# One PSUM pool and one side of SBUF kept through the MLP of a one-layer trunk, with four pairs' first products ahead

## The chip, the core and the metric

The kernel runs on one core of a Trainium2 chip. The metric is the device time of the program in microseconds (us): the median of three runs before the change was 1617.08 us (1616.24 to 1624.27). Five engines work side by side: TensorE (PE, matmuls), VectorE (DVE), ScalarE (ACT), GpSimd (POOL) and SyncE (SP, which issues most DMA transfers). Each has its own queue and takes its instructions in order; semaphores hold an instruction back until what it reads is written and what it overwrites has been read. Data lies in SBUF (128 partitions), sums of matmuls in PSUM (8 banks of 128 x 512 floats).

## The reference

One layer over 1024 tokens of 1024 features, with an MLP of 4096 features between:

```
h = rmsnorm(x) * (1 + sc1) + sh1
o = concat(stick_breaking_attention(h), sparse_attention(h))    # each group normalised
x = x + ga1 * (o @ w_out)
h = rmsnorm(x, g_mlp) * (1 + sc2) + sh2
x = x + ga2 * (square(relu(h @ w_up)) @ w_down)
return rmsnorm(x, g_final)
```

The shifts, scales and gates come from `silu(c) @ w_mod + b_mod`. The change lies in the last three lines: between the output projection `o @ w_out` and the end of the MLP.

## The kernel before

All products run in pieces of float32: an operand is split into a high part (ACT copies it into a rounded type, L158) and a low part (DVE or POOL subtracts, L159), and each product is three matmuls, high x high, high x low, low x high.

*Output projection and second norm.* `out_tile` takes 128 tokens at a time, in the order 6, 7, 4, 5, 2, 3, 0, 1: matmuls into two PSUM tiles, DVE adds `x` (L998), ACT squares and sums (L999), SP stores the tile to DRAM (`x1d`), POOL computes the reciprocal root, and DVE multiplies the tile by it in place (L1004); the statistics stand in a small tile `st`. `h2_pair` transposes two tiles on PE into PSUM tiles `x2T` (L1030), ACT brings each out with scale and shift into eight tiles `h2f` of features x tokens (L1034), and the columns of tokens 512 to 1023 are split at once into `h2h` and `h2l`. `h2_sums` then forms, for 256 token columns at a time, four sums and differences of quarters of the activations: `s1` on POOL (L1054), three differences on DVE (L1055 to L1057).

*Up product.* The product with `w_up` runs over 16 pairs `p` of two tiles of 128 output features. For each pair the 2 x 2 block product (two halves of 1024 inputs, two of the tokens) is done in seven half-size products instead of eight, each of 4 x 3 = 12 matmuls of 128x128 by 128x512. Their activation operands are `11`, `12` (from `h2h`, `h2l`), `s1`, `s2`, `s3`, `s4` and `22`, split at the head of the MLP part (names `hs`, `hs1`, `h22`) for columns 256 to 511 first and 0 to 255 last. Their weight operands come from two loads per pair, `wrup{p}_0` (blocks 11, 21) and `wrup{p}_1` (12, 22); DVE forms four differences in place in the loaded blocks (L1183, L1184, L1188, L1190), and ACT and POOL split six or seven blocks of 128x512. The first two products (`up_first`: 11 by 11, then 21 by 12, into the same bank `upa`) need no difference. Between the two, ACT copies the bank out (`p1`, in the trace `p`, L93). The five others (`up_rest`: `upb` with t2, t3, t4 and `upd` with t1 and 22) do; DVE adds `p1` to them (L1210, `u` and `c`), ACT applies relu and square, and the results go to DRAM (`ud`). In program order pairs 0 and 1 do their `up_first` first, then pair 0 its `up_rest`; from pair 2 on, the pieces of one pair's `up_first` alternate with those of the pair before. `gate_piece` meanwhile computes the gate `ga2` from `w_mod` on SP and DVE (`m3raw`, two buffers).

*Down product.* Eight groups of 4 feature tiles read `ud` and `w_down` back, split both, and for each of 8 token tiles x 2 halves do 12 matmuls into a bank `dn` (L177 to L179); DVE adds it (L1347). The last group adds the final norm.

*What sets the order.* The program is written through a tile framework: a scheduler places each instruction in its engine's queue by data, buffers and priorities (`early`, with `PRI`), and a pool gives each tag a number of buffers, so that a tile waits until the one that had its buffer has been read. Around the change, the attention's PSUM pool `psb` (tags z, tr, av: 4, 3 and 1 banks) is closed and a pool `psc` (A, B, D: 4, 2, 2) is opened, and SBUF pool `bq` is closed after the activation splits and `gq` opened in its place.

## Time and profile before

| | us | share |
|---|---|---|
| median of 3 runs | 1617.08 | |
| the profiled execution | 1617.77 | |
| its span | 1616.0 | 100% |
| PE busy (matmuls) | 1438.5 | 89% |
| PE weight loads, beside the matmuls | 1181.8 | 73% |
| DVE busy | 1096.7 | 68% |
| ACT busy | 756.3 | 47% |
| POOL busy | 655.0 | 41% |

The span runs from the first to the last instruction; 1.77 us of the execution lie around it. A matmul's record is longer than the distance to the next one, since matmuls are pipelined. Idle time on PE is what the program pays for where PE is the limit; idle time elsewhere costs nothing. Rows of the timeline give in brackets how long the engine was idle before, and whose work ended that.

### The profile page before, as it was taken

Reading aid. Unit: us, or ns where it says so; the run is one execution under the profiler, and the core shown is the slowest. Engines: PE = TensorE matmul, PEld = TensorE weight load, DVE = VectorE, ACT = ScalarE, POOL = GpSimd, SP = SyncE. Lnnn points to the kernel's source line nnn. Section 1 sums busy time; section 2 is a strip of 40 time slices with the busy share of each in tenths; the row PEclk is TensorE's granted clock in tenths of the full one; section 3 lists DMA queues with packets and bytes.
Section 4 is the critical chain, followed back from the end, with each engine's and each line's share of the span. In section 5 each row is a group of like instructions: output and inputs, shape, how many; then the busy total and the mean of one; then the engine's idle time right before and its main releaser. Section 6 shows DMA issues by size and latency. Waiting matters only on the chain.

```text
span 1616.0 us, 20016 instructions
## 1 busy us (share of the span) xinstructions
PE 1438.5 (89%) x7056; PEld 1181.8 (73%) x7056; DVE 1096.7 (68%) x1950; ACT 756.3 (47%) x1474; POOL 655.0 (41%) x489
## 2 busy tenths in 40 slices
PE   4879968887798778999999778999999999999998
PEld 3658747666686657888788656788788788888886
DVE  7878999999957885999644655352335657566534
ACT  5766465433445545888733543445445212121112
POOL 3343223433436556675552564445443222222101
PEclk8999968888799879999989889999999999999999
DMA  9531221322111212211312134344335623223102
GB/s 327 150 92 41 72 53 40 102 69 91 34 40 40 69 56 86 92 60 53 102 56 104 53 98 143 115 134 128 126 124 202 234 78 122 87 93 105 64 7 98
DMA packets 118213, 155.08 MB, mean 96 GB/s; under 512 B 9520, under 2 KB 77144, under 8 KB 118112
## 3 DMA queue, kind: packets, MB, share of 16 engines
q1 hardware_dynamic: 108464, 136.98, 27.0%
q10 hardware_dynamic: 9648, 16.81, 2.8%
q8 instruction: 56, 0.92, 0.2%
q14 instruction: 45, 0.37, 0.1%
HBM read 116.52 MB, written 33.05 MB: 93 GB/s over the span
## 4 chain that ended last, share of the span: by engine, by line
PE 55%; DVE 27%; DMA 5%; issue 5%; ACT 4%; POOL 3%; SPq 0%; DVEq 0%; POOLq 0%; ACTq 0%
PE dn L178 7%; PE dn L179 7%; PE dn L177 7%; DVE tk_jk L504 4%; DVE tk_jk L530 4%; DVE m L710 4%; PE upb L1199 2%; PE upb L1201 2%; PE upb L1200 2%; DVE m2acc L403 2%; DMA wrup<-in_w_up_dram 2%; DMA wm<-in_w_mod_dram 2%; PE avd L645 2%; PE upd L1200 2%; PE upd L1201 2%
## 5 line engine op out<-in xcount | busy, mean ns | idle before, releaser
L178 PE MATMUL dn<-wld,uh 128*128 128x512 f32 x512 | 201.7, 394 | 0.0
L179 PE MATMUL dn<-whd,ul 128*128 128x512 f32 x512 | 201.6, 394 | 0.0
L177 PE MATMUL dn<-whd,uh 128*128 128x512 f32 x512 | 199.7, 391 | 1.8 <-DVE x L1347 1.8
L173 POOL TENSOR_TENSOR wld<-wrd,whd 128x1024 fp32r<-128x1024 f32 x32 | 81.5, 2557 | 238.5 <-ACT whd L172 223.6
L712 POOL TENSOR_TENSOR be<-be,m 128x895 f32<-128x895 f32 (+7 forms) x64 | 89.4, 1400 | 171.5 <-DVE m L710 111.8
L1347 DVE TENSOR_TENSOR x<-dn,x 128x512 f32<-128x512 f32 x128 | 86.6, 685 | 100.9 <-PE dn L179 100.9
L710 DVE TENSOR_TENSOR_SCAN m<-m 128x896 f32<-128x896 f32 (+7 forms) x64 | 98.7, 1548 | 28.6 <-ACT m L708 26.2
L177 PEld LDWEIGHTS dn<-whd,uh 128*128 128x128 f32 x512 | 97.5, 190 | 23.6 <-DVE x L1347 2.2
L178 PEld LDWEIGHTS dn<-wld,uh 128*128 128x128 f32 x512 | 96.5, 189 | 21.1
L172 ACT ACTIVATE whd<-wrd 128x1024 fp32r<-128x1024 f32 x32 | 33.8, 1056 | 166.3 <-PE dn L178 83.8
L179 PEld LDWEIGHTS dn<-whd,ul 128*128 128x128 f32 x512 | 96.6, 189 | 20.1
L159 POOL TENSOR_TENSOR w<-wrup,w 128x512 fp32r<-128x512 f32 x48 | 62.9, 1315 | 118.3 <-ACT w L158 118.3
L159 POOL TENSOR_TENSOR wt<-wrup,wt 128x512 fp32r<-128x512 f32 x64 | 85.6, 1364 | 19.3 <-ACT wt L158 19.3
L159 DVE TENSOR_TENSOR ul<-ur,uh 128x512 fp32r<-128x512 f32 x64 | 79.2, 1261 | 18.2 <-ACT uh L158 16.0
L530 DVE TENSOR_SCALAR_CACHE_REDUCE tk_jk<-mk,tlo,above 128x384 bf16<-128x384 uint16 (+4 forms) x80 | 74.7, 934 | 2.0
L645 PE MATMUL avs<-wts,va 128*128 128x256 f32 (+1 forms) x320 | 56.3, 305 | 19.7 <-DVE ota L663 10.0
L171 DVE TENSOR_TENSOR wrd<-wrd,gate 128x1024 f32<-128x1024 f32 x32 | 47.2, 1476 | 36.6 <-DMA wrd<-in_w_down_dram 36.6
L504 DVE TENSOR_SCALAR_CACHE_REDUCE tk_jk<-mk,thr 128x384 bf16<-128x384 bf16 (+4 forms) x80 | 70.0, 875 | 1.2
L158 ACT ACTIVATE uh<-ur 128x512 fp32r<-128x512 f32 x64 | 37.6, 620 | 69.7 <-PE dn L178 54.5
L645 PEld LDWEIGHTS avs<-wts,va 128*128 128x128 f32 x320 | 48.1, 205 | 26.1 <-DVE ota L663 9.5
L822 POOL TENSOR_TENSOR dl<-dl,dst 128x896 f32<-128x896 f32 (+4 forms) x40 | 51.2, 1296 | 34.7 <-DVE dst L818 24.7
L158 ACT ACTIVATE w<-wrup 128x512 fp32r<-128x512 f32 x48 | 29.7, 626 | 75.4 <-DMA wrup<-in_w_up_dram 40.2
(386 smaller groups left out, 4471.6 us busy)
## 6 DMA issues: line engine op xcount, KB each, us to landing
wrup<-in_w_up_dram SPq DMA_DIRECT2D x32, 512.0 KB, 5.5
ur<-ud SPq DMA_DIRECT2D x32, 512.0 KB, 3.3
wrd<-in_w_down_dram SPq DMA_DIRECT2D x32, 512.0 KB, 4.4
m2raw<-in_w_mod_dram SPq DMA_DIRECT2D x24, 512.0 KB, 4.3
ud<-c ACTq DMA_DIRECT2D x48, 256.0 KB, 2.1
wm<-in_w_mod_dram SPq DMA_DIRECT2D x24, 256.0 KB, 6.0
x<-in_x_dram SPq DMA_DIRECT2D x8, 512.0 KB, 6.3
wrdq<-in_w_in_dram SPq DMA_DIRECT2D x8, 512.0 KB, 4.8
```

Source lines behind the costliest of these rows:

```text
L158: A.activation(hi, src, AF.Copy)
L159: (lo_eng or V).tensor_tensor(lo, src, hi.bitcast(F32), op=OP.subtract)
L173: (lo_eng or G).tensor_tensor(lo, raw, hi.bitcast(F32), op=OP.subtract)
L177: T.matmul(ps, ah, bh, start=start, stop=False)
L178: T.matmul(ps, ah, bl, start=False, stop=False)
L179: T.matmul(ps, al, bh, start=False, stop=stop)
L504: V.tensor_scalar(jk[:, :widths[b]], src or sc[b], t, 0.5 - TOPK, op0=op, op1=OP.add, accum_out=c)
L530: V.tensor_scalar(jk[:, :widths[b]], mk[b].bitcast(U16), tlo[:, j:j + 1], above[:, j:j + 1], op0=OP.is_ge, op1=OP.add, accum_out=cnt[0][:, ...
L645: T.matmul(dst, vv, rhs, start=kt == 0 and l == 0, stop=half and l == 1)
L710: V.tensor_tensor_scan(m[:, :n][:, ::-1], m[:, :n][:, ::-1], m[:, :n][:, ::-1], 1.0, op0=OP.mult, op1=OP.bypass)
L712: G.tensor_tensor(be[:, :n - 1], be[:, :n - 1], m[:, 1:n], op=OP.mult)
L1347: V.tensor_tensor(xc, ps, xc, op=OP.add)
```

## The change

The PSUM pool `psb` and the SBUF pool `bq` now live to the end of the program. The MLP's banks use the attention's tags (`upa` and `dn` z, `upb` tr, `upd` tr and av in turn), and its SBUF tiles use tags of `bq` (`wt`, `kl`, `wkL`, `ot`, `sc3`, `mk7`, `jk`, `h2f`), some with fewer buffers: three `s` instead of four, one `m3raw` instead of two, the low parts of the down product in four tiles. The statistics `st` move to `bq`. The last token tile is normalised into a tile of its own, `xn`. `s1` is summed on DVE; the low halves of `k = 1` of the first-split columns stay on POOL, those of the second half go to DVE. With `LEAD = 4` the first products of pairs 0 to 3 come ahead of everything else of the up product, from a first load of their block; the block is loaded a second time (`"b"`) for the differences. For pair 4 the first products come after pair 3's rest, and from pair 5 on they alternate as before.

```diff
--- before.py
+++ after.py
@@ -191,11 +191,10 @@
     DVE_BLOCKS, ACT_BLOCKS = TKB
     hTh, hTl = {}, {}
     widths = {b: P * (b + 1) for b in range(NB)}
-    bq_guard = tc.tile_pool(name="bqpool", bufs=1, side="right")
-    bq = bq_guard.__enter__()
+    bq = ctx.enter_context(tc.tile_pool(name="bqpool", bufs=1, side="right"))
+    pp = ctx.enter_context(tc.tile_pool(name="psb", bufs=1, space=PSUM))
     with ExitStack() as pctx:
         bp = pctx.enter_context(tc.tile_pool(name="bpool", bufs=1))
...
-            st = bp.tile([P, 4], F32, tag="st", bufs=4, name=f"h2st{tt}")
+            st = bq.tile([P, 4], F32, tag="st", bufs=4, name=f"h2st{tt}")
...
             V.tensor_tensor(st[:, 0:1], st[:, 2:3], st[:, 3:4], op=OP.add)
             rstd(st[:, 1:2], st[:, 0:1], D)
-            V.tensor_scalar(xt, xt, st[:, 1:2], None, op0=OP.mult)
-            return xt
+            xn = bq.tile([P, S], F32, tag="wt", bufs=WT, name=f"xn{tt}") if tt == 1 else xt
+            V.tensor_scalar(xn, xt, st[:, 1:2], None, op0=OP.mult)
+            return xn
 
...
-                G.tensor_tensor(s1, a21, a22, op=OP.add)
+                V.tensor_tensor(s1, a21, a22, op=OP.add)
...
-        pp = pctx.enter_context(tc.tile_pool(name="psc", bufs=1, space=PSUM, reuse_waits="tile"))
...
-                    split(ah[nm, k][:, ts], al[nm, k][:, ts], f(k)[:, ts], A, G if k % 2 else V)
-        bq_guard.__exit__(None, None, None)
-        gq = pctx.enter_context(tc.tile_pool(name="gqpool", bufs=1, side="right", reuse_waits="tile"))
+                    split(ah[nm, k][:, ts], al[nm, k][:, ts], f(k)[:, ts], A, G if k == 3 or (c and k == 1) else V)
 
         def bank(tag, name):
-            return pp.tile([P, 512], F32, tag=tag, bufs=4 if tag == "A" else 2, name=name)
-
-        def otile(name):
-            return gq.tile([P, 512], F32, tag="o", bufs=12, name=name)
+            return pp.tile([P, 512], F32, tag=tag, bufs={"z": ZB, "tr": TRB, "av": AVB}[tag], name=name)
+
+        def spare(p, name):
+            return bq.tile([P, 512], F32, tag=("mk7", "jk", "h2f")[p % 3], bufs=1, name=name)
...
 
-        def w_ops(p):
-
-            raw = []
-            for u in range(2):
-                t_ = (gp if u else wp).tile([P, KT, P], F32, tag="wro" if u else "wr", bufs=2, name=f"wrup{p}_{u}")
-                SY.dma_start(t_, wu[:, :, (2 * p + u) * P:(2 * p + u + 1) * P])
-                raw.append(t_)
+        def w_split(nm, src, p, pool, tag, n):
+            t_ = pool.tile([P, 2, 4, P], F32R, tag=tag, bufs=n, name=f"w{nm}_{p}")
+            split(t_[:, 0], t_[:, 1], src, A, G)
+            return t_
+
+        def w_load(p, u, again=""):
+            t_ = (gp if u else wp).tile([P, KT, P], F32, tag="wro" if u else "wr", bufs=2, name=f"wrup{p}_{u}{again}")
+            SY.dma_start(t_, wu[:, :, (2 * p + u) * P:(2 * p + u + 1) * P])
+            return t_
+
+        def w_first(p, t_):
+            return {"11": w_split("11", t_[:, 0:4, :], p, wp, "wh", WHB),
+                    "21": w_split("21", t_[:, 4:8, :], p, wp, "wl", WLB)}
+
+        def w_rest(p, raw, ops):
+
             b11, b21, b12, b22 = raw[0][:, 0:4, :], raw[0][:, 4:8, :], raw[1][:, 0:4, :], raw[1][:, 4:8, :]
-            ops = {}
-
-            def operand(nm, src, pool, tag, n):
-                t_ = pool.tile([P, 2, 4, P], F32R, tag=tag, bufs=n, name=f"w{nm}_{p}")
-                split(t_[:, 0], t_[:, 1], src, A, G)
-                ops[nm] = t_
-
-            operand("11", b11, wp, "wh", WHB)
-            operand("21", b21, wp, "wl", WLB)
             V.tensor_tensor(b11, b12, b11, op=OP.subtract)
             V.tensor_tensor(b12, b22, b12, op=OP.subtract)
-            operand("t3", b12, gp, "s", 4)
-            operand("t1", b11, gq, "s2", 6)
-            operand("22", b22, gq, "s2", 6)
+            ops["t3"] = w_split("t3", b12, p, gp, "s", 3)
+            ops["t1"] = w_split("t1", b11, p, bq, "wkL", WL)
+            ops["22"] = w_split("22", b22, p, bq, "kl", KL)
             V.tensor_tensor(b22, b22, b11, op=OP.subtract)
-            operand("t2", b22, gp, "s", 4)
+            ops["t2"] = w_split("t2", b22, p, gp, "s", 3)
             V.tensor_tensor(b21, b21, b22, op=OP.subtract)
-            operand("t4", b21, gq, "s2", 6)
-            return ops
+            ops["t4"] = w_split("t4", b21, p, bq, "wkL", WL)
...
         def up_first(p, ops, r):
 
-            if p == 0:
-                r["b"], r["d"] = bank("B", f"upb{p}"), bank("D", f"upd{p}")
-            ps = bank("A", f"upa{p}")
+            ps = bank("z", f"upa{p}")
             product(ps, "11", "11", ops, True)
-            p1 = r["p1"] = gp.tile([P, 512], F32, tag="p1", bufs=2, name=f"p1_{p}")
+            p1 = r["p1"] = gp.tile([P, 512], F32, tag="p1", bufs=4, name=f"p1_{p}")
             early("ev", A.activation, p1, ps, AF.Copy)
             yield
             product(ps, "21", "12", ops, False)
-            c = otile(f"c11_{p}")
+            c = spare(p, f"c11_{p}")
             early("ev", A.activation, c, ps, AF.Relu)
             A.activation(c, c, AF.Square)
             A.dma_start(ud[2 * p][:, 512:1024], c)
@@ -1227,22 +1221,20 @@
 
         def up_rest(p, ops, r):
             p1 = r["p1"]
-            if p:
-                r["b"], r["d"] = bank("B", f"upb{p}"), bank("D", f"upd{p}")
-            b_, d_ = r["b"], r["d"]
+            b_, d_ = bank("tr", f"upb{p}"), bank("av" if p % 2 else "tr", f"upd{p}")
             product(b_, "t2", "s2", ops, True)
-            u2 = otile(f"u2_{p}")
+            u_ = bq.tile([P, 2, 512], F32, tag="wt", bufs=WT, name=f"u_{p}")
+            u2, u3 = u_[:, 0], u_[:, 1]
             ev_add(u2, b_, p1)
             product(d_, "t1", "s1", ops, True)
             product(b_, "t3", "s3", ops, False)
-            u3 = otile(f"u3_{p}")
             ev_add(u3, b_, p1)
             yield
             product(b_, "t4", "22", ops, False)
-            c22 = otile(f"c22_{p}")
+            c_ = bq.tile([P, 2, 512], F32, tag="wt", bufs=WT, name=f"c_{p}")
+            c22, c21 = c_[:, 0], c_[:, 1]
             ev_add(c22, d_, u3)
             finish(c22, 2 * p + 1, 0)
-            c21 = otile(f"c21_{p}")
             ev_add(c21, b_, p1)
             finish(c21, 2 * p, 0)
...
-            raw = gq.tile([P, 2, 512], F32, tag="gate", bufs=2, name=f"m3raw{c}_{k2}")
+            raw = bq.tile([P, 2, 512], F32, tag="ot", bufs=OTB, name=f"m3raw{c}_{k2}")
...
-        prev = []
+
+        LEAD = 4
+        rs = {p: {} for p in range(NPR)}
+        firsts = {}
+        for p in range(LEAD):
+            for _ in up_first(p, w_first(p, w_load(p, 0)), rs[p]):
+                pass
         for p in range(NPR):
-            ops, r = w_ops(p), {}
+            raw = [w_load(p, u, "b" if p < LEAD else "") for u in range(2)]
+            if p < LEAD:
+                ops, lead = {}, None
+            else:
+                ops = w_first(p, raw[0])
+                lead = up_first(p, ops, rs[p])
+            w_rest(p, raw, ops)
             if 2 <= p < 12:
                 gates[p - 2]()
-            first, rest = up_first(p, ops, r), up_rest(p, ops, r)
-            if p < 2:
-                for _ in first:
+            rest = up_rest(p, ops, rs[p])
+            if p < LEAD:
+                for _ in rest:
                     pass
+            elif p == LEAD:
+                for _ in lead:
+                    pass
+                prev = rest
             else:
-                old = prev.pop(0)
-                next(old)
-                next(first)
-                next(old)
-                next(first)
-                next(old)
-            prev.append(rest)
-            if p == 1:
-                for _ in prev.pop(0):
-                    pass
-        for _ in prev[0]:
+                next(prev)
+                next(lead)
+                next(prev)
+                next(lead)
+                next(prev)
+                prev = rest
+        for _ in prev:
             pass
 
...
         WD = ((wp, "wh", WHB), (wp, "wl", WLB), (wp, "wh", WHB), (wp, "wl", WLB),
-              (gp, "s", 4), (gp, "s", 4), (gp, "s", 4), (gp, "s", 4))
+              (gp, "s", 3), (gp, "s", 3), (gp, "s", 3), (bq, "kl", KL))
...
                         if hf:
                             t_ = gp.tile([P, S], F32R, tag="t", bufs=12, name=f"uh{ft}")
-                        uh[f, hf] = t_[:, cs]
-                        ul[f, hf] = gq.tile([P, 512], F32R, tag="o", bufs=12, name=f"ul{ft}_{hf}")
+                            t2_ = bq.tile([P, S], F32R, tag="wt", bufs=WT, name=f"ul{ft}")
+                        uh[f, hf], ul[f, hf] = t_[:, cs], t2_[:, cs]
                     split(uh[f, hf], ul[f, hf], ur[:, cs])
```

Three places show what moves. The first is PE's queue from the last transposes of token tiles 0 and 1 to the first product of `up_rest`. `x2T0_k` are the transposes (`xr0`, `xr1`, `xn1` the normalised tiles 0 and 1), `upa0` the bank of pair 0's first products, each block of 12 matmuls shown by its first row. Before:

```order
L1030 MATMUL x2T0_2_8765<-ident_72,xr0_8579 128x128
L1030 MATMUL x2T0_0_8751<-ident_72,xr1_8642 128x128
...
L1030 MATMUL x2T0_3_8772<-ident_72,xr1_8642 128x128
L1199 MATMUL upa0_8946<-h2h0_1_8346,w11_0_8919 128x512
...
L1199 MATMUL upa1_9006<-h2h0_1_8346,w11_1_8981 128x512
...
L1199 MATMUL upa0_8946<-h2h4_1_8380,w21_0_8922 128x512
...
L1199 MATMUL upa1_9006<-h2h4_1_8380,w21_1_8984 128x512
...
L1199 MATMUL upd0_8945<-hs1h0_8827,wt1_0_8930 128x512
...
L1199 MATMUL upb0_8944<-hs2_0_8803,wt2_0_8937 128x512
```

After:

```order
L1030 MATMUL x2T0_2_8766<-ident_72,xr0_8579 128x128
L1195 MATMUL upa0_8916<-h2h0_1_8346,w11_0_8910 128x512
...
L1195 MATMUL upa1_8955<-h2h0_1_8346,w11_1_8949 128x512
...
L1030 MATMUL x2T0_0_8752<-ident_72,xn1_8702 128x128
...
L1030 MATMUL x2T0_2_8766<-ident_72,xn1_8702 128x128
L1195 MATMUL upa0_8916<-h2h4_1_8380,w21_0_8913 128x512
...
L1195 MATMUL upa2_8994<-h2h0_1_8346,w11_2_8988 128x512
...
L1195 MATMUL upa1_8955<-h2h4_1_8380,w21_1_8952 128x512
...
L1030 MATMUL x2T0_3_8773<-ident_72,xn1_8702 128x128
...
L1195 MATMUL upa3_9033<-h2h0_1_8346,w11_3_9027 128x512
...
L1195 MATMUL upb0_9087<-hs2_0_8800,wt2_0_9080 128x512
...
L1195 MATMUL upd0_9088<-hs1h0_8824,wt1_0_9073 128x512
```

The first products of pairs 0 and 1 now stand ahead of the transposes of tile 1, pairs 2 and 3 follow behind pair 0's second product, and `upb0` comes after eight products of 12 matmuls, where `upd0` came after four.

The second place is DVE's queue from the normalisation of token tile 1 (L1004) to the sums of the last 256 columns (L1055) and the weight differences of pair 0 (L1183 and on before, L1180 and on after). `hs` are low halves of activation operands, `h2s` the sums `s1`, `wrup0_0b` the block loaded a second time. Before:

```order
L1004 TENSOR_SCALAR xr1_8642<-xr1_8642,h2st1_8692 128x1024
L159 TENSOR_TENSOR hs2_0_8803<-h2f0_8344,hs2_0_8803 128x256
...
L1183 TENSOR_TENSOR wrup0_0_8915<-wrup0_1_8917,wrup0_0_8915 128x512
...
L1184 TENSOR_TENSOR wrup0_1_8917<-wrup0_1_8917 128x512
...
L1184 TENSOR_TENSOR wrup1_1_8979<-wrup1_1_8979 128x512
L1055 TENSOR_TENSOR h2f0_8344<-h2f0_8344 128x256
L1056 TENSOR_TENSOR h2f0_8344<-h2s0_8733,h2f0_8344 128x256
L1055 TENSOR_TENSOR h2f1_8350<-h2f1_8350 128x256
L1057 TENSOR_TENSOR h2f4_8378<-h2f4_8378,h2f0_8344 128x256
```

After:

```order
L1004 TENSOR_SCALAR xn1_8702<-xr1_8642,h2st1_8692 128x1024
L159 TENSOR_TENSOR hs2_2_8806<-h2f2_8361,hs2_2_8806 128x256
...
L1054 TENSOR_TENSOR h2s0_8734<-h2f0_8344,h2f4_8378 128x256
L1054 TENSOR_TENSOR h2s0_8734<-h2f1_8350,h2f5_8384 128x256
L1055 TENSOR_TENSOR h2f0_8344<-h2f0_8344 128x256
...
L1180 TENSOR_TENSOR wrup0_0b_9064<-wrup0_1b_9066,wrup0_0b_9064 128x512
...
L1181 TENSOR_TENSOR wrup0_1b_9066<-wrup0_1b_9066 128x512
L1180 TENSOR_TENSOR wrup1_0b_9165<-wrup1_1b_9167,wrup1_0b_9165 128x512
...
L159 TENSOR_TENSOR hs3_2_8818<-h2f2_8361,hs3_2_8818 128x256
L1185 TENSOR_TENSOR wrup0_1b_9066<-wrup0_1b_9066,wrup0_0b_9064 128x512
```

Before, the differences of pairs 0 and 1 stand ahead of the sums of the last columns; after, the sums `s1` (L1054) come first and the differences stand among and behind them.

The third place is POOL's queue in the same stretch: `h22`, `hs1`, `hs3` and `hs4` are low halves of activation operands, `w11_2` the low half of pair 2's block 11, `wt1`, `w22`, `wt2`, `wt3` those of the differences. Before:

```order
L1054 TENSOR_TENSOR h2s0_8733<-h2f0_8344,h2f4_8378 128x256
L1054 TENSOR_TENSOR h2s0_8733<-h2f1_8350,h2f5_8384 128x256
L159 TENSOR_TENSOR wt3_0_8927<-wrup0_1_8917,wt3_0_8927 128x512
...
L159 TENSOR_TENSOR h22l1_8848<-h2f5_8384,h22h1_8847 128x256
L159 TENSOR_TENSOR hs1l1_8832<-h2s0_8733,hs1h1_8831 128x256
...
L159 TENSOR_TENSOR hs3_1_8818<-h2f1_8350,hs3_1_8818 128x256
...
L159 TENSOR_TENSOR hs4_3_8868<-h2f7_1_8401,hs4_3_8868 128x256
L159 TENSOR_TENSOR wt1_0_8930<-wrup0_0_8915,wt1_0_8930 128x512
L159 TENSOR_TENSOR w22_0_8933<-wrup0_1_8917,w22_0_8933 128x512
L159 TENSOR_TENSOR wt2_0_8937<-wrup0_1_8917,wt2_0_8937 128x512
```

After:

```order
L159 TENSOR_TENSOR hs4_3_8865<-h2f7_1_8401,hs4_3_8865 128x256
L159 TENSOR_TENSOR w11_2_8988<-wrup2_0_8986,w11_2_8988 128x512
L159 TENSOR_TENSOR w22_0_9076<-wrup0_1b_9066,w22_0_9076 128x512
L159 TENSOR_TENSOR w11_3_9027<-wrup3_0_9025,w11_3_9027 128x512
L159 TENSOR_TENSOR w21_2_8991<-wrup2_0_8986,w21_2_8991 128x512
L159 TENSOR_TENSOR w21_3_9030<-wrup3_0_9025,w21_3_9030 128x512
L159 TENSOR_TENSOR h22l3_8853<-h2f7_0_8732,h22h3_8852 128x256
...
L159 TENSOR_TENSOR wt1_0_9073<-wrup0_0b_9064,wt1_0_9073 128x512
L159 TENSOR_TENSOR w22_1_9177<-wrup1_1b_9167,w22_1_9177 128x512
...
L159 TENSOR_TENSOR wt3_0_9070<-wrup0_1b_9066,wt3_0_9070 128x512
...
L159 TENSOR_TENSOR wt2_0_9080<-wrup0_1b_9066,wt2_0_9080 128x512
```

The sums of `s1` and most low halves of activations are gone from there, and the low halves of pairs 2 and 3's first blocks stand ahead of those of pair 0's differences.

## Rows read from the trace of the kernel before

**Rows 1.** The page's second part: PE's busy tenths in 40 slices.

```profile
PE   4879968887798778999999778999999999999998
```

**Rows 2.** Table of stretches: us, then PE, PEld, DVE, ACT, POOL, clock, DMA, GB/s.

```profile
909.60:919.00 9.40, 0.26 (x3) 0.02 (x1) 6.03 (x13) 5.21 (x17) 5.28 (x8) 0.63 0.39 108
929.70:939.50 9.80, 0.00 (x0) 0.00 (x0) 9.80 (x18) 4.72 (x13) 6.32 (x8) 0.65 0.00 0
946.60:1010.00 63.40, 57.84 (x248) 46.06 (x247) 31.53 (x36) 25.50 (x47) 36.12 (x27) 1.00 0.46 135
1010.00:1250.00 240.00, 240.00 (x1041) 194.63 (x1040) 95.98 (x131) 118.20 (x205) 110.91 (x83) 1.00 0.42 136
```

**Rows 3.** Timeline of PE, 919 to 1007: start, us, instruction, idle before and its releaser.

```profile
919.01 2.18 PE L1030 MATMUL x2T<-ident,xr 128*128 128x128 f32 x9 [9.16 <-DVE xr L1004]
...
939.52 0.79 PE L1199 MATMUL upa<-h2h,w 128*128 128x512 f32 x1 [9.84 <-ACT p L93]
940.11 0.63 PE L1200 MATMUL upa<-h2l,w 128*128 128x512 f32 x1
...
942.67 0.46 PE L1200 MATMUL upa<-h2l,w 128*128 128x512 f32 x1
...
946.64 0.40 PE L1199 MATMUL upd<-hs1h,wt 128*128 128x512 f32 x1
...
961.91 0.50 PE L1199 MATMUL upb<-h22h,wt 128*128 128x512 f32 x1 [0.84 <-DVE u L1210]
...
977.94 0.50 PE L1199 MATMUL upb<-hs,wt 128*128 128x512 f32 x1 [2.69 <-DVE u L1210]
...
987.93 0.50 PE L1199 MATMUL upb<-h22h,wt 128*128 128x512 f32 x1 [0.96 <-DVE u L1210]
...
1006.49 0.50 PE L1199 MATMUL upb<-h22h,wt 128*128 128x512 f32 x1 [1.07 <-DVE u L1210]
```

**Rows 4.** Timeline of DVE, 905 to 941.

```profile
905.74 2.96 DVE L1057 TENSOR_TENSOR h2f<-h2f,h2f 128x256 f32<-128x256 f32 x2
...
913.82 0.68 DVE L998 TENSOR_TENSOR xr<-wo,xr 128x512 f32<-128x512 f32 x1
...
918.03 0.93 DVE L1004 TENSOR_SCALAR xr<-xr,h2st 128x1024 f32<-128x1024 f32 x1 [2.58 <-DMA x1d<-xr]
...
927.08 0.95 DVE L1055 TENSOR_TENSOR h2f<-h2f 128x256 f32<-128x256 f32 x1
...
935.91 0.41 DVE L1055 TENSOR_TENSOR h2f<-h2f 128x256 f32<-128x256 f32 x1
...
939.66 0.75 DVE L159 TENSOR_TENSOR hs<-h2f,hs 128x256 fp32r<-128x256 f32 x2
```

**Rows 5.** Table of stretches, columns as in rows 2: the last columns' sums and splits.

```profile
927.00:940.50 13.50, 3.66 (x14) 2.71 (x13) 13.37 (x23) 7.09 (x19) 9.26 (x12) 0.71 0.00 0
```

**Rows 6.** Timeline of ACT, 915 to 924.

```profile
915.16 2.24 ACT L158 ACTIVATE hs<-h2f 128x256 fp32r<-128x256 f32 x7
...
919.05 1.64 ACT L158 ACTIVATE hs<-h2f 128x256 fp32r<-128x256 f32 x5 [1.65 <-DVE xr L1004]
920.60 2.82 ACT L1034 ACTIVATE h2f<-x2T,modT,A 128x256 f32<-128x256 f32 x6
```

**Rows 7.** Timeline of POOL, from 905.5.

```profile
905.54 2.87 POOL L159 TENSOR_TENSOR w<-wrup,w 128x512 fp32r<-128x512 f32 x2 [0.68 <-ACT w L158]
```

**Rows 8.** Waits of DVE, 946 to 1010: us in total, times, longest.

```profile
DVE wrup L1183 <- POOL w L159: 18.3, 4, 9.5
```

**Rows 9.** Tile wrup, 890 to 990: duration in ns min/median/max, times; DMA at the end.

```profile
L158 ACT ACTIVATE wt<-wrup x14: 612/620/633, 923.5 to 976.8; 128x512 fp32r<-128x512 f32 x14
L159 POOL TENSOR_TENSOR wt<-wrup,wt x14: 1280/1305/1755, 924.9 to 977.5; 128x512 fp32r<-128x512 f32 x14
L1183 DVE TENSOR_TENSOR wrup<-wrup,wrup x5: 1209/1762/1771, 920.8 to 984.2; 128x512 f32<-128x512 f32 x5
DMA to landing us min/median/max: 4.8/5.5/6.1
```

More of the change, by code (lines that the diff above doesn't have):

```diff
@@ L193, in tile_trunk @@
     widths = {b: P * (b + 1) for b in range(NB)}
-    bq_guard = tc.tile_pool(name="bqpool", bufs=1, side="right")
-    bq = bq_guard.__enter__()
+    bq = ctx.enter_context(tc.tile_pool(name="bqpool", bufs=1, side="right"))
+    pp = ctx.enter_context(tc.tile_pool(name="psb", bufs=1, space=PSUM))
     with ExitStack() as pctx:
         bp = pctx.enter_context(tc.tile_pool(name="bpool", bufs=1))
-        pp = pctx.enter_context(tc.tile_pool(name="psb", bufs=1, space=PSUM))
         def ztile(name):
@@ L269, in tile_trunk @@
                 xt = xs[tt]
-                st = bp.tile([P, 2], F32, tag="st", bufs=4, name=f"xst{tt}")
+                st = bq.tile([P, 2], F32, tag="st", bufs=4, name=f"xst{tt}")
                 jk = bp.tile([P, D], mybir.dt.uint8, tag="jka", bufs=1, name=f"xjk{tt}")
@@ L731, in kv_half @@
             A.activation(kf, ps, AF.Copy)
-            st = bp.tile([P, 4], F32, tag="st", bufs=4, name=f"kvst{hf}")
+            st = bq.tile([P, 4], F32, tag="st", bufs=4, name=f"kvst{hf}")
             rs = pjtile(f"kvrs{hf}")
@@ L961, in norm_b @@
             rs = pjtile(f"rsb{i}")
-            st = bp.tile([P, 4], F32, tag="st", bufs=4, name=f"nstb{i}")
+            st = bq.tile([P, 4], F32, tag="st", bufs=4, name=f"nstb{i}")
             row_rstd(rs[:, 0:256], rs[:, 508:512], [sqb[hf][:, ts], sq], 512, st)
@@ L1263, in gate_piece @@
                 if k2 == 0 and u == 0:
-                    macc[c] = otile(f"m3acc{c}")
+                    macc[c] = bq.tile([P, 512], F32, tag="sc3", bufs=1, name=f"m3acc{c}")
                     V.tensor_scalar(macc[c], raw[:, 0, :], ck, None, op0=OP.mult)
@@ L1269, in gate_finish @@
         def gate_finish(c):
-            ps = bank("A", f"m3ps{c}")
-            row = otile(f"m3row{c}")[0:1, :]
+            ps = bank("z", f"m3ps{c}")
+            row = spare(c, f"m3row{c}")[0:1, :]
             SY.dma_start(row, b_mod[None, 5120 + 512 * c:5632 + 512 * c])
@@ L1328, in tile_trunk @@
                             t_ = gp.tile([P, S], F32R, tag="t", bufs=12, name=f"uh{ft}")
-                        uh[f, hf] = t_[:, cs]
-                        ul[f, hf] = gq.tile([P, 512], F32R, tag="o", bufs=12, name=f"ul{ft}_{hf}")
+                            t2_ = bq.tile([P, S], F32R, tag="wt", bufs=WT, name=f"ul{ft}")
+                        uh[f, hf], ul[f, hf] = t_[:, cs], t2_[:, cs]
                     split(uh[f, hf], ul[f, hf], ur[:, cs])
             if fg == NG - 1:
-                gfin = gq.tile([P, D], F32, tag="gate", bufs=2, name="gfin")
+                gfin = bq.tile([P, D], F32, tag="ot", bufs=OTB, name="gfin")
                 SY.dma_start(gfin, g_final[None, :].to_broadcast([P, D]))
@@ L1342, in tile_trunk @@
                     xc = x1[tt, ch]
-                    ps = bank("A", f"dn{fg}_{tt}_{ch}")
+                    ps = bank("z", f"dn{fg}_{tt}_{ch}")
                     for f in range(FFG):
@@ L1349, in tile_trunk @@
                         if ch == 0:
-                            st = gq.tile([P, 3], F32, tag="st2", bufs=4, name=f"fst{tt}")
-                            y = gq.tile([P, D], F32, tag="s2", bufs=6, name=f"y{tt}")
+                            st = bq.tile([P, 3], F32, tag="st", bufs=4, name=f"fst{tt}")
+                            y = bq.tile([P, D], F32, tag="wkL", bufs=WL, name=f"y{tt}")
                         A.activation(y[:, cs], xc, AF.Square, accum_out=st[:, ch:ch + 1])
```

2 lines of the change are left out of this document (1 added, 1 removed).

## The prediction, made before the changed kernel ran

> **What bounds the kernel now.** I read the page's slices first, then a table of stretches around the change, then the tensor engine's timeline there, and last the queues of the engines it waits for. The slices, of 40.4 us each, show a tensor engine (PE) that is 0.4 to 0.9 busy in the first sixteen, 0.9 in the next six, 0.7, 0.7 and 0.8 from 889 to 1010 us, and 0.9 from there to the last [rows 1]. The change leaves the first sixteen alone, so only the dip at 889 to 1010 can pay. The table says the same with edges: PE is busy 0.26 of 9.4 us after the output projection and 0 of 9.8 us a little later, 57.84 of 63.4 us in the ramp of the up product, and all of 240 us in its steady part [rows 2]. In the timeline the losses are: 9.16 us until the last token tile is normalised, 9.84 us until ACT has copied the first product of pair 0 or 1 out of PSUM (`p`), and 0.84, 2.69, 0.96 and 1.07 us in the ramp, each until a DVE addition `u` [rows 3]. After each long wait PE restarts at half clock: 0.43 us from matmul to matmul (940.11 to 942.67, six of them) [rows 3] against 240/1041 = 0.23 us in the steady part [rows 2].
>
> What those long waits hang on is DVE. From 927.08 to 940.41 it runs 22 instructions on 256 columns back to back, the sums and splits of the second half of the token columns [rows 4], and the ACT copies that PE waits for stand in ACT's queue behind splits that need these sums.
>
> **The change, part by part.**
> *Products ahead.* By the moment at which the first `up_rest` product starts (946.64, `upd` [rows 3]) the kernel before has done the two first products of two pairs, 4 x 12 = 48 matmuls. The new one does eight such products, 96 matmuls, before its `upb0`. So if the first `up_rest` product starts at a time T in the new kernel, PE has 48 matmuls less left at T: 48 x 0.23 = 11.1 us. The gain is 11.1 + (946.6 - T) + the ramp's stalls of before - the ramp's stalls of after - one restart at half clock (0.20 us more for each of about 7 matmuls, 1.4 us).
>
> *T.* In the new order `upb0` waits for `t2` of pair 0: POOL's low half behind ACT's high half behind DVE's L1185. On DVE 31 instructions stand from the first sum of the second half to that one, 27 of 256 columns and 4 of 512, where before there were 22 and none: the four sums and five low halves (`k = 1`) taken from POOL, and four weight differences, which before stood ahead of the half. They start when ACT has brought up the fifth `h2f` tile. ACT: the 12 `hs` splits begin at 915.16 as before and no longer stop for the statistics tile in the middle (1.65 us [rows 6]); 12 x 2.24/7 = 3.8, so 919.0; then five instructions new in this place (`p` of pairs 0 and 1, three weight splits) at 0.62 [rows 9], 3.1 us, so 922.1; five `h2f` at 2.82/6 = 0.47 [rows 6], so 924.4, against 927.08. This step takes the same start for the last tile's addition (913.82 [rows 4]); the four sums of the first half that come onto DVE before it take the place of POOL's, which ran beside it, and I cost them at nothing. The 2.58 us for which the normalisation waited for the store of x1 [rows 4] goes with the separate tile `xn`, but ACT's queue, not this, sets the start.
>
> A 256-column instruction took 13.37/23 = 0.58 us in that stretch, while POOL worked 9.26 us in 12 instructions beside it, 0.40 us for each of DVE's [rows 5]. In the new order POOL has seven splits of 512 (1.305 [rows 9]) and four of 256 (9.26/12 = 0.77) beside the 31, 12.2 us or 0.39 each, so I keep 0.58: 27 x 0.58 = 15.7. The 512-column differences go at 1.21, the least that one took beside POOL [rows 9]: 4.8. So L1185 ends at 924.4 + 20.5 = 944.9, and `t2` is there 0.62 + 1.31 later [rows 9]: T = 946.8, where it was. Bounds: with every 256 at 0.41, as alone [rows 4], 941.8; with each DVE instruction held as those two were that stood beside a 512-wide POOL split, 2.96/2 = 1.48 [rows 4, 7], and 1.77 for the wide ones [rows 9], 27 x 1.48 + 4 x 1.77 = 47.0, so 973.3. I take 946.8, by the stretch that is most like it.
> The Trainium skill, SBUF — State Buffer, section Who interferes with whom, speaks against the change: an instruction of VectorE with two SBUF inputs and one of GpSimd that reads SBUF exclude each other, and whoever comes second is blocked for the other's whole length. The trace agrees where it shows 0.95 and 0.41 us for a subtraction of one shape [rows 4], but POOL is not busy all the time; held to the letter with a POOL that never rests, the rule gives the 973.3, and that is a rival below.
>
> *The ramp.* Before, its stalls were 0.84 + 2.69 + 0.96 + 1.07 = 5.6 us [rows 3]. They come from additions `u` behind L1183, which waits for POOL's splits of the block it overwrites: 18.3 us in four waits [rows 8]. For the first four pairs these splits are gone from that place, since the block is loaded a second time; L1183 waits for that load instead, 5.5 us from its issue [rows 9]. The second load needs the buffer of pair 2 or 3, free once POOL has split it, about 927 by the above, so it lands at about 932, near the place where DVE comes to it. Against that, in the ramp no first products stand between a pair's own, `m3raw` has one buffer and not two, and SP's queue holds the second loads of pairs 2 and 3 behind it, with the additions `u3` behind both on DVE. Bounds: no stall, or four of the largest seen (2.69), 10.8 us. I take half of what there was, 2.8 us.
>
> *At nothing.* The four extra loads (0.5 MB each): the DMA engines moved nothing from 929.7 to 939.5 and were 46% busy in the ramp [rows 2]. Fewer buffers in the steady part (three `s`, one `m3raw`, two `wt` tiles a pair): 24 to 36 other matmuls (5.5 to 8.3 us) lie between a buffer's release and its next use in PE's order, against 1.9 us for ACT and POOL to refill it; without that cover each pair would cost those 1.9 us. The down product keeps one set of tiles for even and one for odd groups, and a group lasts 192 x 0.23 = 44 us. PSUM: 8 banks before and after, each pair's reused two pairs later. Everything up to the last two token tiles keeps its order.
>
> **Sum.** 11.1 + (946.6 - 946.8) + 5.6 - 2.8 - 1.4 = 12.3 us. The profiled execution took 1617.77 (span 1616.0 and 1.77 around it), so 1605.5; the median of the runs is 0.69 lower, so I forecast **1604.8**.
>
> **Rivals.**
> 1. The ramp starves: four pairs' products stand back to back, and the additions `u` wait behind `m3raw` and the second loads. For it: all four short stalls of before are of this kind [rows 3], and one buffer fewer. Against it: 13.8 us of PE work a pair (60 matmuls) against 6.5 us on POOL (five splits). Price 10.8 instead of 2.8: 1612.8, no change that can be told.
> 2. The shared port decides: `t2` of pair 0 comes at 973.3 and the time is 1604.8 + 26.5 = 1631, slower. For it the 1.48 us and 1.77 us rows [rows 4, 7, 9]. Against it: POOL has 12 us of work in that stretch, not 47. It wipes the gain out from T = 959, and makes the kernel measurably slower from T = 967.
> 3. The refill shows: `t2` now has the same buffer for every pair, and if its split stood in the open in the 12 later pairs it would cost 12 x 1.9 = 23 us: 1628. Against it the cover above.
> 4. It goes better: T = 941.8 and no stalls in the ramp, 7.8 us more: 1597.
>
> **How the numbers follow.** What a measurement of this kernel can tell from no change is about 0.5%, 8 us: 1609.0 to 1625.2. Chances: the forecast (1599 to 1609) 0.60, rival 4 0.12, rival 1 0.19, rival 2 0.06, rival 3 0.03. So faster 0.72, same 0.19, slower 0.09. The range takes in rivals 4 and 1 and leaves out the other two and a few hundredths below: 1596 to 1613.
>
> **What would show it.** In the profile after: 24 matmuls `upa` straight after the last output projection, before the nine transposes, where 9.16 us of waiting stood; one wait of about 8 us before the first `upb`, which starts near 947 after 96 `upa` matmuls; its releaser ACT or POOL `wt`; DVE busy almost without a break before it; less than 6 us of PE idle from there to the steady part, and the down product beginning about 12 us earlier than before. Wrong if the first `upb` starts after 955 (DVE beside POOL is dearer than 0.58), if PE waits more than 3 us a pair in the ramp (rival 1), or if it is idle in the steady part (rival 3).

## The result, and the profile after

The changed kernel took 1600.31 us (median of 4, 1597.82 to 1602.25) against 1616.66 before: a ratio of 0.9889 with a 95% interval of 0.9855 to 0.9923. Run again in two later sets it stood at 0.9881 (0.9860 to 0.9903) and 0.9881 (0.9861 to 0.9901). The forecast was 1604.8 us, in a range of 1596 to 1613: right in sign and range, too small in size.

The timed runs scatter by 2 to 3 us, and the profiles show where: the last output matmul starts at 909.8, 907.1 and 911.6 us in three profiles of the changed kernel, but from there to the first matmul of the down product all three take 321.3 to 321.4 us. So the parts are compared by two stretches of the profiled executions:

| | last output matmul | first `dn` | between | first `dn` to end of span |
|---|---|---|---|---|
| before | 909.14 | 1245.10 | 335.96 | 370.89 |
| after | 909.80 | 1231.15 | 321.35 | 364.95 |

14.6 us went between the two products and 5.9 in the down product and tail, 20.5 in all. The medians of the three sets moved by 16 to 19; the rest is probably the scatter ahead of these stretches, but of the kernel before there is only one profile.

PE's timeline of the changed kernel, at the places that answer to [rows 3]:

```profile
917.49 0.33 PE L1030 MATMUL x2T<-ident,xn 128*128 128x128 f32 x1 [1.48 <-DVE xn L1004]
...
932.45 0.50 PE L1195 MATMUL upa<-h2h,w 128*128 128x512 f32 x1 [2.34 <-ACT p L93]
...
939.65 0.50 PE L1195 MATMUL upb<-hs,wt 128*128 128x512 f32 x1 [1.30 <-ACT wt L158]
939.99 0.40 PE L1196 MATMUL upb<-hs,wt 128*128 128x512 f32 x1
940.22 0.39 PE L1195 MATMUL upd<-hs1h,wt 128*128 128x512 f32 x1
...
942.95 0.79 PE L1197 MATMUL upd<-hs1h,wt 128*128 128x512 f32 x1 [2.10 <-POOL wt L159]
943.55 0.63 PE L1195 MATMUL upd<-hs1h,wt 128*128 128x512 f32 x1
...
949.74 0.80 PE L1197 MATMUL upb<-hs,wt 128*128 128x512 f32 x1 [2.15 <-POOL wt L159]
...
964.66 0.50 PE L1195 MATMUL upb<-h22h,wt 128*128 128x512 f32 x1 [1.35 <-DVE u L1206]
```

The waits of 9.16 and 9.84 us are 1.48 and 2.34; the four of the ramp are three others, two of them for low halves that POOL makes. `upb` starts with the two matmuls that read only the high half of t2 (L1195, L1196); its third (L1197) needs the low half and comes at 949.74. DVE and then POOL in the same stretch, for [rows 4 and 7]:

```profile
923.95 1.99 DVE L1054 TENSOR_TENSOR h2s<-h2f,h2f 128x256 f32<-128x256 f32 x2 [2.14 <-ACT h2f L1034]
...
933.43 0.68 DVE L1180 TENSOR_TENSOR wrup_0b<-wrup_1b,wrup_0b 128x512 f32<-128x512 f32 x1
...
938.25 0.68 DVE L1185 TENSOR_TENSOR wrup_1b<-wrup_1b,wrup_0b 128x512 f32<-128x512 f32 x1
...
939.46 0.75 DVE L1057 TENSOR_TENSOR h2f<-h2f,h2f 128x256 f32<-128x256 f32 x2
940.85 0.93 DVE L1257 TENSOR_SCALAR m3acc<-m3raw,c_act 128x512 f32<-128x512 f32 x1 [0.64 <-POOL h22l L159]
```

```profile
932.78 8.03 POOL L159 TENSOR_TENSOR h22l<-h2f,h22h 128x256 fp32r<-128x256 f32 x1 [2.57 <-ACT h22h L158]
940.77 0.72 POOL L159 TENSOR_TENSOR hs1l<-h2s,hs1h 128x256 fp32r<-128x256 f32 x1
941.45 1.45 POOL L159 TENSOR_TENSOR wt<-wrup_0b,wt 128x512 fp32r<-128x512 f32 x1
```

One POOL instruction on 256 columns, 0.72 us for its neighbour, stood for 8.03 us and ended 0.6 us after DVE's first pause, at 940.21; DVE's instructions meanwhile took 0.41 and 0.68 us. The low half of t1, whose source DVE had ready at 934.1 (the L1180 row), came at 942.9, and PE waited for it.

The down product's groups of 192 matmuls hold the second half of the story. First matmuls of groups 1 to 4 before:

```profile
1301.36 0.39 PE L177 MATMUL dn<-whd,uh 128*128 128x512 f32 x1
...
1345.72 0.39 PE L177 MATMUL dn<-whd,uh 128*128 128x512 f32 x1
...
1389.25 0.39 PE L177 MATMUL dn<-whd,uh 128*128 128x512 f32 x1
...
1433.61 0.39 PE L177 MATMUL dn<-whd,uh 128*128 128x512 f32 x1
```

The odd groups 1 and 3 take 44.36 us, group 2 takes 43.53, with no wait in any of them. In the changed kernel each takes 43.52. The odd groups read other tiles than the even ones, which led to the first experiments.

### The profile page after: what moved, and what is told of

Its sections match the earlier page's. It is cut to its first block, busy times and chain, and to the rows that moved or that the text cites. A ratio compares the mean times of both kernels' runs of the same rounds, so it can differ in the third digit from the quotient of the medians.

```text
span 1596.1 us, 20085 instructions
## 1 busy us (share of the span) xinstructions
PE 1439.3 (90%) x7056; PEld 1186.3 (74%) x7056; DVE 1117.3 (70%) x1963; ACT 761.3 (48%) x1474; POOL 657.7 (41%) x476
## 4 chain that ended last, share of the span: by engine, by line
PE 57%; DVE 28%; DMA 4%; ACT 4%; issue 4%; POOL 3%; SPq 0%; DVEq 0%; POOLq 0%; ACTq 0%
PE dn L177 7%; PE dn L178 7%; PE dn L179 7%; DVE tk_jk L503 4%; DVE tk_jk L529 4%; DVE m L709 4%; PE upb L1195 3%; PE upb L1197 3%; PE upb L1196 3%; DMA wm<-in_w_mod_dram 2%; PE wo L177 2%; PE wo L178 2%; PE upd L1195 2%; PE upd L1197 2%; PE upd L1196 2%
## 5 line engine op out<-in xcount | busy, mean ns | idle before, releaser
L159 DVE TENSOR_TENSOR ul<-ur,uh 128x512 fp32r<-128x512 f32 x64 | 84.0, 1342 | 22.2 <-ACT uh L158 19.3
L159 POOL TENSOR_TENSOR wt<-wrup,wt 128x512 fp32r<-128x512 f32 x48 | 66.9, 1399 | 44.2 <-ACT wt L158 41.7
L552 ACT ACTIVATE tk_jka<-sc,thr 128x1024 uint8<-128x1024 f32 x32 | 37.0, 1156 | 57.9 <-DVE thr L559 49.2
```

The source lines that it names most:

```text
L159: (lo_eng or V).tensor_tensor(lo, src, hi.bitcast(F32), op=OP.subtract)
```

## The experiments

**Addresses: b_align, a_align, a_align2, a_left.** In the built programs, the low part `ul` of an odd group (stationary operand, brought in by PE's weight load) lies at 210784 before and 215008 after, its `w_down` part `whd` (moving operand, read by the matmul itself) at 93920 in both: 913 and 946 times 128 bytes apart. The same holds for the products t1, t4 and 22: odd multiples before; after, 22's became even. The small statistics tiles (4 x 32 bytes) shift whatever is laid beside them by 128.

```diff
-                            st = gq.tile([P, 3], F32, tag="st2", bufs=4, name=f"fst{tt}")
+                            st = gq.tile([P, 3], F32, tag="st2", bufs=8, name=f"fst{tt}")
```

> The kernel before, with eight buffers of 32 bytes for the last statistics tile instead of four, which moves every other tile of the MLP's right-hand pool by 128 bytes; the order of all engines is unchanged. Theory A (address): three matmuls of a product take 0.693 to 0.699 us instead of 0.680 to 0.683 wherever the stationary operand's address and the moving operand's differ by an odd multiple of 128 bytes. Then the odd groups of the down product go from 0.693 to 0.680 per three (256 x 0.013 = 3.3 us), t1, t4 and 22 from 0.698 to 0.683 (192 x 0.015 = 2.9 us), and the kernel from 1616.7 to 1610.5. Rival B (traffic): the slower pace of every second group comes from what the other engines and the DMAs do beside it; then nothing moves: 1616.7.

1607.68 us, 0.9951 (0.9934 to 0.9969) of the kernel before: 8.3 us from 128 bytes that nothing uses. Every group is now fast, 43.52 us:

```profile
1294.84 0.39 PE L177 MATMUL dn<-whd,uh 128*128 128x512 f32 x1
...
1338.36 0.39 PE L177 MATMUL dn<-whd,uh 128*128 128x512 f32 x1
...
1381.88 0.39 PE L177 MATMUL dn<-whd,uh 128*128 128x512 f32 x1
```

Three matmuls of t1, t4 and 22 went from 0.698 to 0.680 us. Traffic is not the cause: instructions and their order are the same. The pace makes 3.3 + 3.3 us (192 x 0.017) of it. A restart at half clock at the head of the down product (8 matmuls, 1.6 us) went too, though the wait of 1.80 us ahead of it stayed; nothing shows that the addresses did that.

```diff
-            st = bq.tile([P, 4], F32, tag="st", bufs=4, name=f"h2st{tt}")
+            st = bq.tile([P, 4], F32, tag="st", bufs=8, name=f"h2st{tt}")
...
```

> The changed kernel with eight statistics buffers instead of four, same order; this moves the tiles of t1 and t4 by 128 bytes and nothing else of the MLP. Theory A: t1 and t4 go from 0.698 to 0.683 us per three matmuls, 128 x 0.015 = 1.9 us: 1598.4 against 1600.3. Rival B: unchanged, 1600.3, with t1 and t4 still at 0.698.

1594.37 us, 0.9868 (0.9850 to 0.9885) of before. Twelve matmuls of t4, from the first row to the second, in the changed kernel (2.79 us) and here (2.72):

```profile
1064.76 0.40 PE L1195 MATMUL upb<-h22h,wt 128*128 128x512 f32 x1
...
1067.55 0.40 PE L1195 MATMUL upa<-h2h,w 128*128 128x512 f32 x1
```

```profile
1063.29 0.39 PE L1195 MATMUL upb<-h22h,wt 128*128 128x512 f32 x1
...
1066.01 0.39 PE L1195 MATMUL upa<-h2h,w 128*128 128x512 f32 x1
```

Three took 0.680 instead of 0.698, as theory A said. The median lies 5.9 us below that of the changed kernel's first set, more than the 1.9 expected; hence a second run beside the changed kernel:

> The changed kernel with eight statistics buffers again, beside the changed kernel on one chip. Address theory: t1 and t4 at 0.681 instead of 0.698 us per three matmuls, 128 x 0.017 = 2.2 us less than the changed kernel of this set. Rival: the lower median of the first time was scatter, no difference.

1593.01 against 1598.57 us, ratios to before 0.9852 (0.9834 to 0.9869) and 0.9881 (0.9861 to 0.9901). The stretch from output to down product is 318.5 us instead of 321.4, 2.9 less, near the 2.2 expected; products right behind t1 and t4 quickened too, from 0.688 to 0.680. The other half of the 5.6 lies outside that stretch, in the two profiles mostly ahead of the last output matmul (907.7 against 911.6), where the changed kernel's own profiles differ by 4.4; whether it belongs to the change is open. This is the fastest version: 24 us below the kernel before in its set.

```diff
-    c_act = cp.tile([P, 8], F32, name="c_act")
+    c_act = cp.tile([P, 8], F32, name="c_act", tag="c_act", bufs=5)
```

> The changed kernel with 128 bytes more of constants at the left end of SBUF, same order: every left-hand tile moves by 128 bytes, the right-hand pool stays. Theory A1 (the difference of the two operands' addresses counts): t1 and t4 become fast (0.683), 22 by s4 becomes slow (0.699), the odd groups of the down product slow (0.693) and the even ones stay near 0.680; time +2.4 to +4 us against the changed kernel. Theory A2 (the stationary operand's own address counts): the even groups, the first products, t2 and t3 all become slow, t1 and t4 stay slow, 22 stays fast; over 7 us more.

It came as A1 said: 22 by s4 0.699, t1 0.680 to 0.689 and t4 0.681, odd groups slow again (44.37 us from the first row to the second, 43.63 for the even one behind):

```profile
1282.86 0.40 PE L179 MATMUL dn<-whd,ul 128*128 128x512 f32 x1
...
1327.23 0.39 PE L179 MATMUL dn<-whd,ul 128*128 128x512 f32 x1
...
1370.86 0.40 PE L179 MATMUL dn<-whd,ul 128*128 128x512 f32 x1
```

It took 1601.58 us (0.9914, 0.9893 to 0.9935), the stretch from the last output matmul to the end 689.4 us, 3.1 more than the 686.3 of the changed kernel's three profiles. What counts is the difference of the two addresses, not either one.

**One part undone: a_psc, a_lead2, a_moves, a_inplace.** The changed kernel, run again, is the measure: after2 (1596.77) beside a_lead2, after3 (1598.57) beside a_moves and a_inplace; a_psc ran in the first set, without it. Where such an edit changes what an instruction waits for, the scheduler places others anew: in a_psc, a_lead2 and a_moves the order of all queues differs from the changed kernel's. They show what the kernel loses without a part, not that part's share alone.

> The changed kernel again, beside the others of this set: both theories 1598 to 1602.

> The changed kernel once more, to stand beside the others of this set: 1596 to 1600.

```diff
-    pp = ctx.enter_context(tc.tile_pool(name="psb", bufs=1, space=PSUM))
...
-        bp = pctx.enter_context(tc.tile_pool(name="bpool", bufs=1))
+        bp = pctx.enter_context(tc.tile_pool(name="bpool", bufs=1)); pp = pctx.enter_context(tc.tile_pool(name="psb", bufs=1, space=PSUM))
...
-        gp = pctx.enter_context(tc.tile_pool(name="gpool", bufs=1, reuse_waits="tile"))
+        gp = pctx.enter_context(tc.tile_pool(name="gpool", bufs=1, reuse_waits="tile")); pp = pctx.enter_context(tc.tile_pool(name="psc", bufs=1, space=PSUM, reuse_waits="tile"))
```

> The changed kernel with the attention's PSUM pool closed before the MLP and a new one of the same tags opened; everything else of the change stays. Theory: without the kept pool the 24 first matmuls cannot stand before the last transposes, so PE waits about 7 us (24 x 0.23 plus the 1.5 it waits now) for the normalised tile, but the start of the first up_rest product is set by DVE and POOL, so the 24 matmuls are made good in the wait before it only as far as there is one (2.3 + 1.3 us): 2 to 4 us slower than the changed kernel, 1602 to 1604. Rival: the kept pool is worth all of the 9 us that went from the wait for the transposes: 1609 or more. Second rival: nothing, 1600.3, since PE waits for the activation splits anyway.

1606.23 us, 0.9939 (0.9922 to 0.9956): 8 to 9 us more than the changed kernel by the ratios, and 331.2 instead of 321.3 in the stretch. PE's waits from 905 to 1012 (us in total, times, longest):

```profile
PE x2T L1030 <- DVE xn L1004: 6.8, 1, 6.8
PE upb L1195 <- DVE u L1206: 5.1, 2, 3.2
PE upa L1197 <- POOL w L159: 3.3, 1, 3.3
PE upa L1195 <- ACT p L93: 2.8, 1, 2.8
PE upb L1195 <- ACT wt L158: 0.9, 1, 0.9
```

My 2 to 4 us was too little: I gave the 24 matmuls back out of the waits of 2.34 and 1.30 us, but waits of 2.8, 3.3 and 0.9 us stand there now. The rival, all of the 9 us, was nearer.

```diff
-        LEAD = 4
+        LEAD = 2
```

> The changed kernel with two pairs' first products ahead instead of four (LEAD = 2). Theory: the start of the first up_rest product is set by DVE and POOL and stays near 939 us, so 48 matmuls less beside it cost 48 x 0.23 = 11.1 us of idle PE, of which at most 3 come back because fewer weight splits stand in ACT's and POOL's queues: 1608 to 1612. Rival: the splits of pairs 2 and 3 are themselves what delays the differences; without them the first up_rest product starts as much earlier, and the kernel stays at 1600.

1604.85 us (0.9929, 0.9912 to 0.9946), 8.1 more than the changed kernel beside it, the stretch 328.4. The size is that of the theory (11.1 less at most 3), the start is the rival's: the first `upb` comes 23.4 us after the last output matmul instead of 29.8. Without the products of pairs 2 and 3 PE idles all the same, 8.62 us before the first `upb` and 3.64 us for POOL's `wt` soon behind it:

```profile
931.41 0.80 PE L1195 MATMUL upb<-hs,wt 128*128 128x512 f32 x1 [8.62 <-ACT hs L158]
...
941.69 0.79 PE L1197 MATMUL upd<-hs1h,wt 128*128 128x512 f32 x1 [3.64 <-POOL wt L159]
```

The weight differences stand ahead of the last columns' sums again (L1180 on DVE at 919.01), so that `upb` waits for a split of the activations (`hs`) and not for t2.

```diff
-                V.tensor_tensor(s1, a21, a22, op=OP.add)
+                G.tensor_tensor(s1, a21, a22, op=OP.add)
...
-                    split(ah[nm, k][:, ts], al[nm, k][:, ts], f(k)[:, ts], A, G if k == 3 or (c and k == 1) else V)
+                    split(ah[nm, k][:, ts], al[nm, k][:, ts], f(k)[:, ts], A, G if k % 2 else V)
```

> The changed kernel with the sums s1 and the low halves of k = 1 given back to POOL. Theory (DVE's unbroken run shuts POOL out, and what waits for POOL waits for the run's end): DVE has nine instructions less there, but its sums now wait for POOL's s1, so DVE and POOL alternate at 0.9 us instead of 0.41; the first up_rest product starts 2 to 6 us later: 2 to 6 us slower than the changed kernel of this set. Rival (DVE's own length decides): nine times 0.34 = 3 us earlier, 3 us faster.

1607.59 us (0.9942, 0.9925 to 0.9959), 9.0 more than the changed kernel beside it and above the 2 to 6 expected, the stretch 330.9. The first `up_rest` product starts 4.8 us later after the last output matmul, as the theory had it; behind it PE waits 10.5 us up to the steady part instead of 5.6, which the theory left out. DVE now waits for POOL's sums and the two alternate; no POOL row is held. DVE, then POOL:

```profile
931.37 0.94 DVE L1055 TENSOR_TENSOR h2f<-h2f 128x256 f32<-128x256 f32 x1 [4.39 <-POOL h2s L1054]
```

```profile
944.26 0.92 POOL L159 TENSOR_TENSOR h22l<-h2f,h22h 128x256 fp32r<-128x256 f32 x1
945.13 1.75 POOL L159 TENSOR_TENSOR wt<-wrup_0b,wt 128x512 fp32r<-128x512 f32 x1
```

```diff
-            xn = bq.tile([P, S], F32, tag="wt", bufs=WT, name=f"xn{tt}") if tt == 1 else xt
+            xn = bq.tile([P, S], F32, tag="wt", bufs=WT, name=f"xn{tt}") if tt == 9 else xt
```

> The changed kernel with the last token tile normalised in place, so that its normalisation waits for the store of x1 as before. Theory: the store lands about 2.4 us after the statistics are there (8.65 us from the last output matmul before, 6.0 now), so the transposes come 2.4 us later, but ACT's queue stands still 2.9 us for a load just before the transposes' tiles; nearly all is absorbed: under 1 us. Rival: the activations' sums wait for it, and the whole 2.4 us show.

1598.69 us (0.9884, 0.9866 to 0.9903), the same as the changed kernel beside it within the scatter, though the stretch is 324.1, 2.8 longer: the wait for the store is back (3.20 us before the transposes), and the first `upb` waits 5.59 us where 1.30 stood. The trace speaks for the rival, the times for the theory: open.

**The ramp: a_low0, a_k3dve.**

```diff
-            split(t_[:, 0], t_[:, 1], src, A, G)
+            f_ = p == 0 and nm in ("t1", "t2"); (early if f_ else lambda k_, g_, *a_: g_(*a_))("ev", split, t_[:, 0], t_[:, 1], src, A, V if f_ else G)
```

> The changed kernel with pair 0's low halves of t1 and t2 taken by DVE instead of POOL. Theory (POOL is held up by DVE's unbroken run): DVE does each in about 0.7 us; the waits of 2.10 and 2.15 us for POOL's wt fall to under 1 us together, and the 22 matmuls at half clock behind them run at full clock: 2 x 2.1 + 22 x 0.2 = 8.6, less what DVE's two more instructions delay: 4 to 8 us less, 1592 to 1596. Rival (the ramp is bound by what follows, the additions u and the second loads): the waits move there and the time stays at 1600.

1602.17 us (0.9913, 0.9890 to 0.9937), 5.4 more than the changed kernel beside it though its runs spread from 1596.8 to 1607.6; the stretch is 325.1: both were wrong. The edit also gives the two splits another priority (`early`). PE's wait for POOL before t1 went. But one instruction more in DVE's run put L1185 0.6 us later, and on ACT the high half of t2 now stands behind a copy `c` that waits for a store, so that PE waits for that high half, and later for DVE's own low half. PE, then ACT:

```profile
941.83 0.52 PE L1195 MATMUL upb<-hs,wt 128*128 128x512 f32 x1 [3.24 <-ACT wt L158]
...
949.14 0.80 PE L1197 MATMUL upb<-hs,wt 128*128 128x512 f32 x1 [2.24 <-DVE wt L159]
```

```profile
940.67 0.60 ACT L93 ACTIVATE c<-upa 128x512 f32<-128x512 f32 x1 [1.35 <-DMA ud<-c]
941.16 1.14 ACT L158 ACTIVATE wt<-wrup_1b 128x512 fp32r<-128x512 f32 x2
```

```diff
-                    split(ah[nm, k][:, ts], al[nm, k][:, ts], f(k)[:, ts], A, G if k == 3 or (c and k == 1) else V)
+                    split(ah[nm, k][:, ts], al[nm, k][:, ts], f(k)[:, ts], A, G if c and k % 2 else V)
```

> The changed kernel with the five low halves that POOL had of the last 256 columns (k = 3) given to DVE; PE's order is the same. Theory (DVE's unbroken run shuts POOL out): the low half of pair 0's t1, now next in POOL's queue, is asked for near 935 us but does not end before DVE's run does, near 942; its row is many us long, and PE's first wait behind upb0 stays at 2 us or grows; time within 2 us of the changed kernel. Rival (POOL's queue is the cause: an 8 us instruction and two more ahead of t1): t1's low half takes 1.3 us, is there by 937, the wait of 2.10 us goes, and 4 to 6 us with it.

1598.86 us (0.9895, 0.9877 to 0.9912), 2.1 more than the changed kernel beside it, within the scatter; the stretch is 322.6. With five instructions more in DVE's run the first `upb` comes 2.0 us later. POOL's queue holds nothing ahead of t1's low half, and yet, from POOL's timeline:

```profile
936.75 7.50 POOL L159 TENSOR_TENSOR wt<-wrup_0b,wt 128x512 fp32r<-128x512 f32 x1 [4.65 <-ACT wt L158]
```

It ends 1.2 us after DVE comes to its first instruction with one input there (`m3acc`, 943.03). So another POOL instruction is held in the same run of DVE's: POOL's queue was not the cause.

## Why the prediction was right, and where its sizes were off

*Right.* The 24 first matmuls stand where 9.16 us were waited; the down product begins 14.0 us earlier (12 forecast); PE waits 5.6 us from the first `upb` to the steady part (under 6); the second loads, the smaller buffers in the steady part and the one t2 buffer cost nothing that shows. a_psc, a_lead2 and a_moves, each with one part back, lose 9.8, 7.0 and 9.5 us of the stretch, more together than the 14.6 that went, as it would be if the parts need one another.

*"I keep 0.58": T.* The step that failed by most, and with it the one wait of 8 us before the first `upb`, which is 2.34 and 1.30. DVE began at 923.95 (924.4 expected; by luck, since ACT's `hs` splits began 2.5 us earlier than I had them and ACT then stood 2.90 us for the load of `wrup_1b`, which I did not have). But its 31 instructions took 15.0 us, not 20.5, since POOL, once held, did not slow them: from then on 0.41 us apiece, and 0.68 for the wide ones that I had at 1.21. The first `up_rest` product starts 29.85 us after the last output matmul where 37.50 stood: 7.65 us gained at T, where the forecast had -0.2. That is 939.0 in the time of the kernel before, below even my lower bound (by its own terms 942.2; the 941.8 is a slip). In a_moves, with POOL among them, a DVE row is back at 0.94.

The path was wrong too: I had T wait for both halves of t2. The first `upb` waited for ACT's high half alone (the 939.65 row), and the low half, 1.31 us behind it in my sum, let `upb` go on only at 949.74. So part of what T gained is waited for in the ramp.

The Trainium skill (SBUF — State Buffer, Who interferes with whom) says that the engine that comes second is blocked for the other's whole instruction. This trace agrees on who is blocked and differs on how long: POOL stood for 8.03 us beside some 18 DVE instructions. Held to the letter against DVE, the rule gave my rival 2; against POOL, and for a run in place of an instruction, it gives what happened. But a run does not always shut POOL out. In the kernel before, POOL's subtractions at 934.12, 936.85 and 938.39, all begun in the course of DVE's run, took 0.73 us each, and the DVE instruction behind was the one that waited. POOL, then DVE:

```profile
934.12 0.73 POOL L159 TENSOR_TENSOR hs<-h2f,hs 128x256 fp32r<-128x256 f32 x1 [1.15 <-ACT hs L158]
```

```profile
934.18 0.94 DVE L159 TENSOR_TENSOR h22l<-h2f,h22h 128x256 fp32r<-128x256 f32 x1
```

What decides between the two no run tells, so why POOL was held in the changed kernel stays open.

*"I take half of what there was, 2.8 us" and 1.4 us of restart.* The ramp lost 2.10 + 2.15 + 1.35 = 5.6 us of waits and 22 x 0.2 = 4.4 us at half clock: 10.0, not 4.2. Two of the three waits, and the half clock behind them, come not from `m3raw` or the second loads, as argued, but from the low halves of t1 and t2 behind POOL's held row; the third is for an addition `u`. A table of the stretch shows the clock (columns as in [rows 2]):

```profile
945.00:957.00 12.00, 9.85 (x27) 7.28 (x26) 7.68 (x7) 4.84 (x9) 12.00 (x10) 0.55 0.45 137
```

0.55 is nearly the lower of the two levels (1.2 of 2.4 GHz), behind the waits of 2.34, 1.30 and 2.10 us. The clock itself was not the price: in another profile of the same kernel (after2) these 12 us ran at 0.86, PE waited 4.19 us instead of 2.15, and the down product came 321.3 us after the output product all the same.

*What the sum left out.* The address pace. With the terms as measured, 11.1 + 7.65 + 5.6 - 10.0 = 14.35, and 22's pace 1.0 (64 x 0.015): 15.3 for the 14.6 measured. In the down product I had nothing; there are 3.3 us for the odd groups (256 x 0.013), the wait of 1.80 that became 0.50, and the restart behind it (1.6): 6.2 for 5.9. Ahead of both, half of the output projection's products lay an odd multiple apart before and none after: 0.693 to 0.683 us for three, 1.3 us (128 x 0.010), which the scatter there hides. That the time fell so near the forecast owes something to luck: T and the ramp were off by 7.85 and 5.8 us in opposite directions, in part because one wait, for t2's low half, moved from the one to the other.
